# k transposed right after its convolution, with its norm, its decayed copy and v's scaling on ScalarE, and weight units in every other step of the down phase

## The chip, the cores and the metric

The kernel runs on one core of one Trainium2 chip. The metric is the device time of one execution in microseconds (us), as the median of several runs. A core has five engines with instruction streams of their own: TensorE (PE in the profile; its weight loads are PEld), VectorE (DVE), ScalarE (ACT), GpSimd (POOL) and SyncE (SP), which here issues nearly all transfers. Each engine and each queue does its instructions in order; semaphores order them against one another. Matrix products go to PSUM, which has eight banks of 128 x 512 float32.

## The reference

One layer of a hybrid decoder trunk on x of 1024 tokens by 1024 features, all in float32: a half SwiGLU feed-forward (FFN, inner width 2816), a mixer, a second FFN and a final norm. The mixer multiplies the normed x by one wide matrix w_in, runs eight GDN heads (gated delta rule, 128 wide) and sixteen Mamba-2 heads over the parts, and projects back with w_out. What matters here is a GDN head:

```python
def l2_normalize(x):
    return x * lax.rsqrt(jnp.sum(x * x, axis=-1, keepdims=True) + EPS)
...
    q = to_chunks(l2_normalize(q) * (dk ** -0.5))
    k = to_chunks(l2_normalize(k))
    v = to_chunks(v)
...
    decay = jnp.exp(jnp.where(incl, gc[..., :, None] - gc[..., None, :], -jnp.inf))
    kk = jnp.einsum("bhcld,bhcsd->bhcls", k, k)
    a_low = jnp.where(strict, beta[..., :, None] * kk * decay, 0.0)
    t_inv = lax.linalg.triangular_solve(eye + a_low, ...)
...
    k_dec = k * jnp.exp(gc[..., -1:] - gc)[..., None]
...
def step(state, inp):
    v_new = u_c - w_c @ state
    o = qd_c @ state + qk_c @ v_new
    state = state * gt_c + k_dec_c^T @ v_new
```

q, k and v come from projections of the normed x, each followed by a causal convolution of four taps and a SiLU. The last lines are abridged.

## The kernel before, in words

**Products.** Each float32 operand is split into a high and a low part of a TensorE format (`split`, L244: a cast on ScalarE, a subtraction on VectorE), and each product is three matmuls. The FFNs and part of the projections use a Strassen-like scheme of seven products on 2 x 2 blocks.

**Stages.** Norm and start, the first FFN's gate and up products, its down phase (about 454 to 660 us), gates and Mamba heads (to about 1000), GDN heads 0 to 7 (about 1000 to 1580), output projection, second FFN. The framework's scheduler orders every engine's instructions by a cost model of its own, so that work of neighbouring stages is interleaved; the order is fixed when the kernel is built.

**The down phase.** Class `Down` walks 42 steps, seven products of six steps. One step is up to 24 matmuls. `Down.prep` (L524) prepares a later step: it loads weight blocks (`wst`, or `keep` for blocks used more than once), loads the hidden activations (`hraw`, from the DRAM tile `hid_scr`), and splits both into `wd` and `hid`. Ahead of that, each call advances `self.side` by one: a generator, `win_units` (L653), that makes the weight units of GDN heads 4 to 7. It loads a column block of w_in (`wraw`), forms sums of its quarters (`wsum`), splits each of seven combinations into a unit (`wunit`) and writes the two halves to DRAM (`wu_scr`, two transfers of 256 KB). Six of eight column blocks are made in the gate and up phase, the last two here, which is fourteen units. At the second product the residual x is loaded (`xtb`, eight transfers of 512 KB). All of these stand in SP's one queue.

**A GDN head.** Heads 0 to 3 project q, k, v and the gate z with ordinary products; heads 4 to 7 do so with `chunk` (L1244), which loads the weight units back (`wunits`, by `unit_load`, L1230, four slots ahead). Then, in the order of the code, with NB = 8 blocks of 128 tokens:

- `kt`, `qt` and `vt_` are the convolved q, k, v, features in partitions, tokens in columns. `conv_from` ends in a SiLU on ScalarE.
- `qe` and `dt` are exponentials of the gates (L1357, L1360), of which each change of function on ScalarE costs a table load.
- For each pair of blocks a PSUM bank of tag `mx` (there are two) takes `kt`'s products with itself and with `qt` (L1372, L1373). VectorE takes the diagonal of the first by a product with the identity (`jd`, L1376), which is the squared norm of each k (`tk`), and then per pair `tk + EPS`, its reciprocal and `br2`. With that it makes `u` (L1383) and `dt` (L1386) out of the bank.
- `vt_` is transposed through `mx`, and VectorE scales it into `vr` (L1412).
- A forward substitution on small blocks follows (`fu`, `fx`, `lv`, L1429 to L1475).
- `kt` is transposed through the two banks of tag `sc` (L1486), and ScalarE scales it by the decay to the end of the chunk, `kd` (L1489, one buffer).
- The recurrence over the blocks (L1498 to L1520), its output norm, and a store `mix_scr` (L1532).

The output projection (`group_tile`, L1557) begins inside the last heads. Its bank copies are `xa` (L1566), its operands `mtt`.

Of the kernel before, what the change touches and what calls it, by code (L numbers as in the profile page):

```python
# [11 lines left out]
F32 = mybir.dt.float32  # L12
# [32 lines left out]
def kernel(  # L45
# [452 lines left out]
    class Down:  # L498
# [23 lines left out]
            return t  # L522

        def prep(self):  # L524
            next(self.side, None)
            if not self.todo:
                return
            m, i, n = self.todo.pop(0)
            c, self.cnt = self.cnt, self.cnt + 1
            raw = wp.tile([P, 2, 2, 512], F32, name="wst", tag="wst")  # L530
            x, *y = W_OPS[m]
            src = self.block(m, x, i, n, raw[:, 0])
            other = self.block(m, y[0], i, n, raw[:, 1]) if y else None
            hraw = hbp[0].tile([P, 2, 512], F32, name="hraw", tag=f"b{3 + c % 3}")
            nc.sync.dma_start(out=hraw[:, 0:n], in_=self.scr[m, i])
            if y:
                V.tensor_tensor(out=raw[:, 0, 0:n], in0=src, in1=other, op=y[1])
                src = raw[:, 0, 0:n]
            w = wp.tile([P, 2, 2, 512], F32R, name="wd", tag=("whi", "wlo")[c % 2])

            th = "b3" if self.tail > 3 and not self.todo else f"b{c % 3}"
            h = hbp[0].tile([P, 2, 2, 512], F32R, name="hid", tag=th)
            split(h[:, 0, 0:n], h[:, 1, 0:n], hraw[:, 0:n])
            self.last = split(w[:, 0, 0:n], w[:, 1, 0:n], src)
            self.ready.append((h, w, n))
# [423 lines left out]
    def token_sums(pool, sq, dst):  # L969

        p = psum("mx")
        for j in range(4):
            T.matmul(p[32 * j:32 * j + 32, 0:256], lhsT=ones[:, 0:32], rhs=sq[:, j * 256:(j + 1) * 256],
                     start=True, stop=True)
        row = pool.tile([P, 256], F32, name="row")
        A.copy(out=row, in_=p[:, 0:256])
        scr = dram.tile([4, 256], F32, name="row_scr", bufs=2)
        nc.sync.dma_start(out=scr, in_=row[0:P:32])
        nc.sync.dma_start(out=dst, in_=scr.rearrange("j (c p) -> p (j c)", p=P))
# [330 lines left out]
    with ExitStack() as cg:  # L1310
        g1 = cg.enter_context(tc.tile_pool(name="gdn1", bufs=1, reuse_waits="tile"))
        g2 = cg.enter_context(tc.tile_pool(name="gdn2", bufs=2, reuse_waits="tile"))
        for h in range(GH):
# [50 lines left out]
            u = g2.tile([P, NB, P], F32, name="u")  # L1364
            tk = g2.tile([P, NB], F32, name="tk")
            br2 = g2.tile([P, NB], F32, name="br2")
            for b0 in range(0, NB, 2):
                pg = psum("mx")
                b2 = slice(b0, b0 + 2)
                for i in range(2):  # L1370
                    bs = slice((b0 + i) * P, (b0 + i + 1) * P)
                    T.matmul(pg[:, i * 256:i * 256 + P], lhsT=kt[:, bs], rhs=kt[:, bs], start=True, stop=True)  # L1372
                    T.matmul(pg[:, i * 256 + P:(i + 1) * 256], lhsT=kt[:, bs], rhs=qt[:, bs],  # L1373
                             start=True, stop=True)
                    jd = g1.tile([P, P], BF16, name="jd")
                    V.scalar_tensor_tensor(out=jd, in0=pg[:, i * 256:i * 256 + P], scalar=1.0, in1=ident,  # L1376
                                           op0=ALU.mult, op1=ALU.mult,
                                           accum_out=tk[:, b0 + i:b0 + i + 1])
                V.tensor_scalar(out=tk[:, b2], in0=tk[:, b2], scalar1=EPS, scalar2=None, op0=ALU.add)
                V.reciprocal(out=br2[:, b2], in_=tk[:, b2])  # L1380
                V.tensor_tensor(out=br2[:, b2], in0=br2[:, b2], in1=beta[:, b2, h], op=ALU.mult)
                for i in range(2):
                    V.scalar_tensor_tensor(out=u[:, b0 + i], in0=pg[:, i * 256:i * 256 + P],  # L1383
                                           scalar=br2[:, b0 + i:b0 + i + 1], in1=dt[:, b0 + i],
# [21 lines left out]
            for half in range(2):  # L1406
                pt = psum("mx")
                for i in range(4):
                    b = half * 4 + i
                    T.transpose(pt[:, i * P:(i + 1) * P], vt_[:, b * P:(b + 1) * P], ident)  # L1410
                hb = slice(half * 4, half * 4 + 4)
                V.tensor_tensor(out=vr[:, hb], in0=pt.rearrange("p (i c) -> p i c", i=4),  # L1412
                                in1=rin[:, hb].unsqueeze(2).to_broadcast([P, 4, P]), op=ALU.mult)


            fs_x = dram.tile([4, NB, 32, 32], F32, name="fs_x", bufs=2)
# [15 lines left out]
            fs_q = fs_x.rearrange("j b (i q) l -> q (j b) i l", q=4)  # L1432
            for q in range(4):
                nc.sync.dma_start(out=fs_q[q], in_=fx[32 * q:32 * q + 32])
            lv = g1.tile([P, 4, 256], F32, name="lv")
            xd, xtr, mt = (lv[:, i].rearrange("p (b l) -> p b l", b=NB) for i in range(3))
            lv2 = g1.tile([P, 2, NB, 64], F32, name="lv2", tag="fu")
            x64, mt2 = lv2[0:64, 0], lv2[:, 1]
# [35 lines left out]
            for b in range(NB):  # L1474
# [1 line left out]
                         start=True, stop=True)  # L1476
            V.tensor_scalar(out=u[0:64, :, 64:128], in0=px[0:64].rearrange("p (b l) -> p b l", b=NB),
                            scalar1=-1.0, scalar2=None, op0=ALU.mult)


            kd = g1.tile([P, NB, P], F32, name="kd")
            for half in range(2):
                pt = psum("sc")
                for i in range(4):
                    b = half * 4 + i
                    T.transpose(pt[:, i * P:(i + 1) * P], kt[:, b * P:(b + 1) * P], ident)  # L1486
                for i in range(4):
                    b = half * 4 + i
                    A.mul(out=kd[:, b], in_=pt[:, i * P:(i + 1) * P], mul=wend[:, b, h:h + 1])  # L1489


            st = None
# [218 lines left out]
```

## Time and profile before

| | |
|---|---|
| median of 3 runs | 2324.86 us (2323.8 to 2327.96) |
| profiled execution | 2323.62 us, span 2321.9 us, mean granted TensorE clock 0.994 |
| TensorE busy | 2268.5 us (98% of the span) |
| VectorE busy | 1777.1 us (77%) |
| ScalarE busy | 1175.0 us (51%) |
| transfers | 356.96 MB, mean 154 GB/s |

TensorE's busy share is near the whole span, so the time is made of what TensorE does, of its few waits, and of stretches in which its granted clock is below 1. In the profile's rows an instruction shows as line, engine, operation and output<-inputs; what stands in brackets behind it is the engine's idle time just before and the instruction or transfer that ended it. SPq is SP's queue of transfers.

### The profile page before, as it was taken

The numbers are of one execution on the slowest core, as the hardware profiler recorded it, in microseconds if no ns is written. First come the engines' busy times: TensorE is split into PE (matmuls) and PEld (weight loads), VectorE is DVE, ScalarE is ACT, GpSimd is POOL, SyncE is SP. The second block draws the span as 40 slices with busy tenths as digits, with TensorE's granted clock in tenths as the row PEclk, the third lists the DMA queues.
The fourth block names the chain that finished last, engine by engine and source line by source line (L and its number), as shares of the span: only waits on it lengthen the run. The fifth ranks groups of instructions, "written<-read, shape, count | busy, mean of one in ns | idle before, by whom it ended". The sixth has DMA issues, their size and how long they took to land.

```text
span 2321.9 us, 32028 instructions
## 1 busy us (share of the span) xinstructions
PE 2268.5 (98%) x11654; PEld 1848.5 (80%) x11654; DVE 1777.1 (77%) x3417; ACT 1175.0 (51%) x2126; POOL 53.0 (2%) x125
## 2 busy tenths in 40 slices
PE   7999999989999999999999999999999999999998
PEld 5788888878878878887787777788878888888886
DVE  8998987768776887667667767678698777766787
ACT  7444433344366986864665566633453333334344
POOL 0000000000000110000000000000000000000000
PEclk9999999999999999999999999999999999999999
DMA  3466662595554433242355556435223333329455
GB/s 111 163 217 236 227 217 97 187 349 177 192 185 138 135 121 100 73 130 65 83 170 165 165 171 182 148 98 191 91 64 123 106 106 110 106 88 353 141 157 213
DMA packets 262195, 356.96 MB, mean 154 GB/s; under 512 B 60809, under 2 KB 167405, under 8 KB 260245
## 3 DMA queue, kind: packets, MB, share of 16 engines
q1 hardware_dynamic: 261780, 354.82, 46.9%
q8 instruction: 91, 1.49, 0.3%
q14 instruction: 68, 0.55, 0.1%
q0 software_dynamic: 256, 0.10, 0.0%
HBM read 249.34 MB, written 105.52 MB: 153 GB/s over the span
## 4 chain that ended last, share of the span: by engine, by line
PE 81%; DVE 7%; ACT 6%; DMA 3%; issue 1%; POOL 0%; SPq 0%; DVEq 0%; ACTq 0%; POOLq 0%
PE ps_pj L123 7%; PE ps_pj L125 7%; PE ps_pj L124 7%; PE ps_pj L334 6%; PE ps_pj L336 6%; PE ps_pj L335 6%; PE ps_mx L334 3%; PE ps_mx L336 3%; PE ps_mx L335 3%; PE ps_pj L559 2%; PE ps_pj L560 2%; PE ps_pj L558 2%; PE ps_oo L334 2%; PE ps_oo L335 2%; PE ps_oo L336 2%
## 5 line engine op out<-in xcount | busy, mean ns | idle before, releaser
L336 PE MATMUL ps_pj<-bh,al 128*128 128x512 f32 x688 | 267.9, 389 | 0.0
L334 PE MATMUL ps_pj<-bh,ah 128*128 128x512 f32 x688 | 267.7, 390 | 0.2 <-ACT m L343 0.2
L335 PE MATMUL ps_pj<-bl,ah 128*128 128x512 f32 x688 | 267.8, 389 | 0.0
L123 PE MATMUL ps_pj<-hhi,whi 128*128 128x512 f32 x576 | 229.9, 399 | 0.4 <-ACT gsb L896 0.4
L125 PE MATMUL ps_pj<-hhi,wlo 128*128 128x512 f32 x576 | 229.4, 398 | 0.0
L124 PE MATMUL ps_pj<-hlo,whi 128*128 128x512 f32 x576 | 228.9, 397 | 0.0
L336 PEld LDWEIGHTS ps_pj<-bh,al 128*128 128x128 f32 x688 | 129.1, 188 | 26.8
L335 PEld LDWEIGHTS ps_pj<-bl,ah 128*128 128x128 f32 x688 | 129.2, 188 | 26.8
L334 PEld LDWEIGHTS ps_pj<-bh,ah 128*128 128x128 f32 x688 | 128.9, 188 | 27.1 <-ACT m L343 0.6
L241 ACT CAST hid<-hraw 128x1024 fp32r<-128x1024 f32 (+1 forms) x84 | 82.3, 981 | 134.6 <-PE ps_oo L560 47.8
L242 DVE TENSOR_TENSOR al<-as,ah 128x512 fp32r<-128x512 f32 x220 | 140.9, 684 | 7.0 <-ACT ah L241 6.5
L317 DVE TENSOR_TENSOR as<-wst 128x512 f32<-128x512 f32 x220 | 144.2, 683 | 2.4 <-DMA wst<-in_ffn_w_up_dram 2.2
L334 PE MATMUL ps_mx<-bh,ah 128*128 128x512 f32 x352 | 138.6, 396 | 5.2 <-ACT sg L380 2.2
L241 ACT CAST ah<-wst 128x512 fp32r<-128x512 f32 x88 | 54.5, 622 | 174.8 <-PE ps_oo L335 112.6
L336 PE MATMUL ps_mx<-bh,al 128*128 128x512 f32 x352 | 137.7, 391 | 1.2 <-DVE al L242 1.2
L335 PE MATMUL ps_mx<-bl,ah 128*128 128x512 f32 x352 | 138.2, 393 | 0.5 <-DVE bl L242 0.5
L241 ACT CAST ah<-as 128x512 fp32r<-128x512 f32 x220 | 125.3, 618 | 20.8 <-DVE as L317 20.8
L123 PEld LDWEIGHTS ps_pj<-hhi,whi 128*128 128x128 f32 x576 | 108.4, 188 | 22.0 <-ACT gsb L896 0.8
L125 PEld LDWEIGHTS ps_pj<-hhi,wlo 128*128 128x128 f32 x576 | 108.4, 188 | 21.3 <-issue 0.9
L124 PEld LDWEIGHTS ps_pj<-hlo,whi 128*128 128x128 f32 x576 | 108.4, 188 | 21.0 <-issue 0.8
L242 DVE TENSOR_TENSOR hid<-hraw,hid 128x1024 fp32r<-128x1024 f32 (+1 forms) x84 | 95.0, 1131 | 23.2 <-ACT hid L241 22.8
L343 ACT COPY m<-ps_pj 128x512 f32<-128x512 f32 x88 | 51.5, 587 | 107.3 <-PE ps_pj L336 105.5
(507 smaller groups left out, 5651.5 us busy)
## 6 DMA issues: line engine op xcount, KB each, us to landing
hraw<-hid_scr SPq DMA_DIRECT2D x70, 512.0 KB, 4.3
wu_scr<-wunit SPq DMA_DIRECT2D x112, 256.0 KB, 3.9
wunits<-wu_scr SPq DMA_DIRECT2D x56, 512.0 KB, 3.9
hid_scr<-hs SPq DMA_DIRECT2D x110, 256.0 KB, 2.6
wst<-in_ffn_w_down_dram SPq DMA_DIRECT2D x50, 512.0 KB, 4.7
wst<-in_ffn_w_gate_dram SPq DMA_DIRECT2D x22, 1024.0 KB, 5.4
wst<-in_ffn_w_up_dram SPq DMA_DIRECT2D x22, 1024.0 KB, 5.5
hid_scr<-sg SPq DMA_DIRECT2D x44, 256.0 KB, 2.0
```

What stands on the lines that cost most here:

```text
L123: T.matmul(o, lhsT=wh, rhs=mh, start=first, stop=False)
L124: T.matmul(o, lhsT=wh, rhs=ml, start=False, stop=False)
L125: T.matmul(o, lhsT=wl, rhs=mh, start=False, stop=last)
L241: return (A.copy(out=hi, in_=src), V.tensor_tensor(out=lo, in0=src, in1=hi.bitcast(F32), op=ALU.subtract))
L242: V.tensor_tensor(out=lo, in0=src, in1=hi.bitcast(F32), op=ALU.subtract))
L317: V.tensor_tensor(out=t, in0=v[0], in1=v[1], op=v[2])
L334: T.matmul(bank, lhsT=wh[:, k], rhs=bh[:, k], start=a, stop=False, skip_group_check=True)
L335: T.matmul(bank, lhsT=wh[:, k], rhs=bl[:, k], start=False, stop=False, skip_group_check=True)
L336: T.matmul(bank, lhsT=wl[:, k], rhs=bh[:, k], start=False, stop=z, skip_group_check=True)
L343: A.copy(out=t, in_=bank)
L558: T.matmul(bank, lhsT=hh, rhs=wh, start=first and k == 0, stop=False, skip_group_check=True)
L559: T.matmul(bank, lhsT=hh, rhs=wl, start=False, stop=False, skip_group_check=True)
```

## The change

It has four parts.

1. `Down.prep` advances the generator of weight units only at every other step.
2. In each GDN head `kt` is transposed through `mx` as soon as it is convolved, ahead of its products. Of each transposed block ScalarE takes the squared norm (a Square with a sum on its output, which gives `tk`) and the decayed copy `kd`, which now has two buffers. `tk + EPS`, its reciprocal and `br2` are computed once for all eight blocks. VectorE's diagonal and the transposes through `sc` are gone.
3. `vr` is scaled on ScalarE, in eight pieces of 128 x 128 instead of two of 128 x 512 on VectorE.
4. The tile `row` of `token_sums` shares its buffer with `fx`, and `lv` has three slots instead of four.

```diff
--- before.py
+++ after.py
@@ -522,7 +522,8 @@
             return t
 
         def prep(self):
-            next(self.side, None)
+            if self.cnt % 2:
+                next(self.side, None)
             if not self.todo:
                 return
             m, i, n = self.todo.pop(0)
@@ -972,7 +973,7 @@
         for j in range(4):
             T.matmul(p[32 * j:32 * j + 32, 0:256], lhsT=ones[:, 0:32], rhs=sq[:, j * 256:(j + 1) * 256],
                      start=True, stop=True)
-        row = pool.tile([P, 256], F32, name="row")
+        row = pool.tile([P, 256], F32, name="row", tag="fx")
         A.copy(out=row, in_=p[:, 0:256])
         scr = dram.tile([4, 256], F32, name="row_scr", bufs=2)
         nc.sync.dma_start(out=scr, in_=row[0:P:32])
@@ -1364,6 +1365,20 @@
             u = g2.tile([P, NB, P], F32, name="u")
             tk = g2.tile([P, NB], F32, name="tk")
             br2 = g2.tile([P, NB], F32, name="br2")
+            kd = g1.tile([P, NB, P], F32, name="kd", bufs=2)
+            for half in range(2):
+                pt = psum("mx")
+                for i in range(4):
+                    b = half * 4 + i
+                    T.transpose(pt[:, i * P:(i + 1) * P], kt[:, b * P:(b + 1) * P], ident)
+                for i in range(4):
+                    b = half * 4 + i
+                    jd = g1.tile([P, P], BF16, name="jd")
+                    A.activation(out=jd, in_=pt[:, i * P:(i + 1) * P], func=AF.Square, accum_out=tk[:, b:b + 1])
+                    A.mul(out=kd[:, b], in_=pt[:, i * P:(i + 1) * P], mul=wend[:, b, h:h + 1])
+            V.tensor_scalar(out=tk, in0=tk, scalar1=EPS, scalar2=None, op0=ALU.add)
+            V.reciprocal(out=br2, in_=tk)
+            V.tensor_tensor(out=br2, in0=br2, in1=beta[:, :, h], op=ALU.mult)
             for b0 in range(0, NB, 2):
                 pg = psum("mx")
                 b2 = slice(b0, b0 + 2)
@@ -1372,13 +1387,6 @@
                     T.matmul(pg[:, i * 256:i * 256 + P], lhsT=kt[:, bs], rhs=kt[:, bs], start=True, stop=True)
                     T.matmul(pg[:, i * 256 + P:(i + 1) * 256], lhsT=kt[:, bs], rhs=qt[:, bs],
                              start=True, stop=True)
-                    jd = g1.tile([P, P], BF16, name="jd")
-                    V.scalar_tensor_tensor(out=jd, in0=pg[:, i * 256:i * 256 + P], scalar=1.0, in1=ident,
-                                           op0=ALU.mult, op1=ALU.mult,
-                                           accum_out=tk[:, b0 + i:b0 + i + 1])
-                V.tensor_scalar(out=tk[:, b2], in0=tk[:, b2], scalar1=EPS, scalar2=None, op0=ALU.add)
-                V.reciprocal(out=br2[:, b2], in_=tk[:, b2])
-                V.tensor_tensor(out=br2[:, b2], in0=br2[:, b2], in1=beta[:, b2, h], op=ALU.mult)
                 for i in range(2):
                     V.scalar_tensor_tensor(out=u[:, b0 + i], in0=pg[:, i * 256:i * 256 + P],
                                            scalar=br2[:, b0 + i:b0 + i + 1], in1=dt[:, b0 + i],
@@ -1408,9 +1416,9 @@
                 for i in range(4):
                     b = half * 4 + i
                     T.transpose(pt[:, i * P:(i + 1) * P], vt_[:, b * P:(b + 1) * P], ident)
-                hb = slice(half * 4, half * 4 + 4)
-                V.tensor_tensor(out=vr[:, hb], in0=pt.rearrange("p (i c) -> p i c", i=4),
-                                in1=rin[:, hb].unsqueeze(2).to_broadcast([P, 4, P]), op=ALU.mult)
+                for i in range(4):
+                    b = half * 4 + i
+                    A.mul(out=vr[:, b], in_=pt[:, i * P:(i + 1) * P], mul=rin[:, b:b + 1])
 
 
             fs_x = dram.tile([4, NB, 32, 32], F32, name="fs_x", bufs=2)
@@ -1432,7 +1440,7 @@
             fs_q = fs_x.rearrange("j b (i q) l -> q (j b) i l", q=4)
             for q in range(4):
                 nc.sync.dma_start(out=fs_q[q], in_=fx[32 * q:32 * q + 32])
-            lv = g1.tile([P, 4, 256], F32, name="lv")
+            lv = g1.tile([P, 3, 256], F32, name="lv")
             xd, xtr, mt = (lv[:, i].rearrange("p (b l) -> p b l", b=NB) for i in range(3))
             lv2 = g1.tile([P, 2, NB, 64], F32, name="lv2", tag="fu")
             x64, mt2 = lv2[0:64, 0], lv2[:, 1]
@@ -1476,17 +1484,6 @@
                          start=True, stop=True)
             V.tensor_scalar(out=u[0:64, :, 64:128], in0=px[0:64].rearrange("p (b l) -> p b l", b=NB),
                             scalar1=-1.0, scalar2=None, op0=ALU.mult)
-
-
-            kd = g1.tile([P, NB, P], F32, name="kd")
-            for half in range(2):
-                pt = psum("sc")
-                for i in range(4):
-                    b = half * 4 + i
-                    T.transpose(pt[:, i * P:(i + 1) * P], kt[:, b * P:(b + 1) * P], ident)
-                for i in range(4):
-                    b = half * 4 + i
-                    A.mul(out=kd[:, b], in_=pt[:, i * P:(i + 1) * P], mul=wend[:, b, h:h + 1])
 
 
             st = None
```

The number of TensorE's instructions stays the same; VectorE has 152 fewer instructions, and ScalarE has eight table loads fewer (66 instead of 74). The scheduler moves instructions on all engines from about the first down phase on. Two places show what moves.

SP's queue in the down phase, around the eight loads of the residual (`xtb`), before:

```order
L535 DMA hraw<-hid_scr_2_0_84 128x1024
L666 DMA wu_scr_169<-wunit 128x512 x2
L521 DMA keep_4235<-in_ffn_w_down_dram 128x2x512
L535 DMA hraw<-hid_scr_2_2_85 128x1024
L578 DMA xtb<-in_x_dram 128x1024 x8
L666 DMA wu_scr_169<-wunit 128x512 x2
L521 DMA keep_4326<-in_ffn_w_down_dram 128x2x512
L535 DMA hraw<-hid_scr_2_4_86 128x1024
L666 DMA wu_scr_169<-wunit 128x512 x2
L658 DMA wraw<-in_w_in_dram 128x8x128 x2
```

and now:

```order
L536 DMA hraw<-hid_scr_2_0_84 128x1024
L667 DMA wu_scr_169<-wunit 128x512 x2
L521 DMA keep_4215<-in_ffn_w_down_dram 128x2x512
L536 DMA hraw<-hid_scr_2_2_85 128x1024
L579 DMA xtb<-in_x_dram 128x1024 x8
L521 DMA keep_4296<-in_ffn_w_down_dram 128x2x512
L536 DMA hraw<-hid_scr_2_4_86 128x1024
L667 DMA wu_scr_169<-wunit 128x512 x2
L521 DMA keep_4296<-in_ffn_w_down_dram 128x2x512
L536 DMA hraw<-hid_scr_2_6_87 128x1024
```

The pair of writes to `wu_scr` behind the `xtb` loads is gone from there, and the load of the next column block, `wraw`, has left this piece. Before, from the end of the gate and up phase on (454 us), five pairs stood ahead of `hraw<-hid_scr_2_4_86`, three of them ahead of this piece; now one does.

ScalarE's stream in the set-up of head 7, before, with the start of v's convolution (`vt_`, L1268), table loads, `qe`, the two SiLUs (`zc` and `vt_`), the exponentials (`dt`, L1360) and the copies `xa` of the output projection:

```order
L1268 ACTIVATE vt__13353<-pre,cols 128x1024
L1264 COPY zc<-ps_pj 128x512
L1348 ACTIVATE zc<-zc 128x1024
L1357 ACT_TABLE_LOAD
L1357 ACTIVATE qe<-dt 128x1024
L1566 ACTIVATE xa<-ps_pj,rg_7158 128x512
L1270 ACT_TABLE_LOAD
L1270 ACTIVATE vt__13353<-vt__13353 128x1024
L1360 ACT_TABLE_LOAD
L1360 ACTIVATE dt<-dt,ngc 128x128 x8
L1566 ACTIVATE xa<-ps_pj,rg_7158 128x512
```

and now, where every line number is one higher up to the exponentials, L1377 are the squares and L1378 the decayed copies:

```order
L1269 ACTIVATE vt__13332<-pre,cols 128x1024
L1265 COPY zc<-ps_pj 128x512
L1358 ACT_TABLE_LOAD
L1358 ACTIVATE qe<-dt 128x1024
L1349 ACT_TABLE_LOAD
L1349 ACTIVATE zc<-zc 128x1024
L1271 ACTIVATE vt__13332<-vt__13332 128x1024
L1361 ACT_TABLE_LOAD
L1361 ACTIVATE dt<-dt,ngc 128x128 x8
L1377 ACTIVATE jd,tk<-ps_mx 128x128
L1378 ACTIVATE kd<-ps_mx,wend 128x128
```

Six of the eight blocks of k are squared and copied ahead of this piece, from the SiLU of `kt` on; one pair of square and copy stands at its end, behind the eight exponentials, and another follows. The copies `xa` have moved behind them. The SiLU of `zc` has moved behind `qe`, to that of `vt_`, and shares its table load.

On TensorE, 37 matmuls of weight units stand at that head between the last matmul of the recurrence before and the eight transposes of k; 24 more, the products of the first pair of blocks, and eighteen matmuls of the output projection stand between those and the products of the second pair.

## The prediction

> **What bounds the kernel.** I began with the page's busy shares and the chain that ended last, since they say which engine's time is the kernel's time.
>
> ```profile
> span 2321.9 us, 32028 instructions
> PE 2268.5 (98%) x11654; PEld 1848.5 (80%) x11654; DVE 1777.1 (77%) x3417; ACT 1175.0 (51%) x2126; POOL 53.0 (2%) x125
> PE 81%; DVE 7%; ACT 6%; DMA 3%; issue 1%; POOL 0%; SPq 0%; DVEq 0%; ACTq 0%; POOLq 0%
> ```
>
> TensorE is idle for 2321.9 − 2268.5 = 53.4 us of the whole program. The change keeps the number of its matmuls and transposes, so it can win only what lies in those idle times and in the slow clock behind them. The view of waits names them; the second and third columns of figures are how many times and the longest one.
>
> ```profile
> PE ps_sc L558 <- ACT hid L241: 5.4, 1, 5.4
> PE ps_mx L1372 <- DVE dt L1386: 3.7, 1, 3.7
> PE ps_pj L1239 <- DMA wunits<-wu_scr: 3.5, 1, 3.5
> PE ps_mx L1372 <- DVE jd L1376: 2.8, 5, 0.9
> ```
>
> The change touches all four places: the first is in the first down phase, the others are in the set-up of the GDN heads. The profiled execution took 2323.62 us, 1.7 more than its span and 1.24 below the median of the three runs; I make the sum against 2323.62 and add 1.24 at the end.
>
> **Part 1: a weight unit every other step of the down phase.** The views of TensorE, ScalarE and of SP's queue in time around the 5.4 us, with the stretches beside them (columns: length, busy time of PE, PEld, DVE, ACT, POOL, granted clock, DMA share, GB/s):
>
> ```profile
> 454.33 1.17 SPq L666 DMA_DIRECT2D wu_scr<-wunit  x2
> ...
> 477.64 9.03 SPq L578 DMA_DIRECT2D xtb<-in_x_dram  x8
> 487.68 1.61 SPq L666 DMA_DIRECT2D wu_scr<-wunit  x2
> 490.24 0.38 SPq L521 DMA_DIRECT2D keep<-in_ffn_w_down_dram  x1
> 491.47 0.32 SPq L535 DMA_DIRECT2D hraw<-hid_scr  x1
> 499.19 1.04 ACT L241 CAST wd<-keep 128x1024 fp32r<-128x1024 f32 x1 [10.16 <-DMA keep<-in_ffn_w_down_dram]
> 500.46 1.04 ACT L241 CAST hid<-hraw 128x1024 fp32r<-128x1024 f32 x1 [0.24 <-DMA hraw<-hid_scr]
> 495.79 0.39 PE L560 MATMUL ps_mx<-wd,hid 128*128 128x512 f32 x1
> 501.56 0.80 PE L558 MATMUL ps_sc<-wd,hid 128*128 128x512 f32 x1 [5.39 <-ACT hid L241]
> 506.96 0.40 PE L558 MATMUL ps_mx<-wd,hid 128*128 128x512 f32 x1
> wu_scr<-wunit SPq DMA_DIRECT2D x112, 256.0 KB, 3.9
> L242 DVE TENSOR_TENSOR wunit<-wsum,wunit 128x512 fp32r<-128x512 f32 x32 | 21.7, 686 | 1.3 <-DMA wu_scr<-wunit 1.2
> 477.60:500.40 22.80, 18.58 (x82) 15.04 (x81) 7.74 (x10) 8.24 (x12) 0.00 (x0) 0.99 1.03 392
> 530.00:610.00 80.00, 80.00 (x355) 66.24 (x354) 64.23 (x72) 28.93 (x31) 0.00 (x0) 1.00 0.49 155
> ```
>
> The stall is a transfer that comes late, not a busy ScalarE: ScalarE sat 10.16 us before the cast of wd and then waited for hraw, and all DMA engines were full (share 1.03). Five pairs of wu_scr writes stand on SP between 454.33 and 487.68 ahead of this hraw. In the changed order one pair of these is left ahead of it, so 4 × 2 × 256 KB = 2.1 MB go later. At 392 GB/s that is 5.35 us: hraw lands at 500.46 − 5.35 = 495.1, the matmul follows as now 501.56 − 500.46 = 1.1 us later, at 496.2. Full-speed pitch is 80.00/355 = 0.225 us, so it is wanted at 495.79 + 0.23 = 496.0, and a stall of 0.2 is left. What the stall costs now is more than 5.39: from 495.79 to 506.96 twelve matmuls start ahead of the last, 13 steps that need 2.9 us at full pitch, and they took 11.17. Gain 8.2; I take **−8.0**. The nearest bound below: were only two of the four pairs of consequence, 2.7 us of wait would be left and about half of the gain, −3. None at all is a rival below.
>
> What is moved comes back between 500 and 610 us, where DMA is at a share of 0.49 and TensorE never waits. VectorE's part of a unit goes there too: a sum and a subtraction of 0.69 each, about 10 us for the seven of the fourteen units that are late; VectorE has 80 − 64.2 = 15.8 us free there. I cost it at 0; it would be 0 to +2 if a write that waits for its unit holds a later hraw in SP's queue, which is in order.
>
> **Part 2: ScalarE takes the norm and the decayed copy; head 7.** Prices first: VectorE's diagonal (L1376), VectorE's scaling of v (L1412), ScalarE's decayed copy (L1489), and ScalarE's square with sum on the output (L1526), the nearest row for the new square of k.
>
> ```profile
> L1376 DVE SCALAR_TENSOR_TENSOR jd<-ps_mx,ident x64: 268/284/292, 1016.1 to 1463.0; 128x128 bf16<-128x128 f32 x64
> L1412 DVE TENSOR_TENSOR vr<-ps_mx,rin x16: 680/691/692, 1029.0 to 1477.5; 128x512 f32<-128x512 f32 x16
> L1489 ACT ACTIVATE kd<-ps_sc,wend x64: 359/371/415, 1081.4 to 1545.3; 128x128 f32<-128x128 f32 x64
> L1526 ACT ACTIVATE jk<-vr x64: 294/310/320, 1084.7 to 1569.8; 128x128 bf16<-128x128 f32 x64
> L1526 ACT ACTIVATION_READ_ACCUMULATOR jk<-vr x64: 185/186/212, 1084.9 to 1570.0; 128x1 f32 x64
> 1010.00:1480.00 470.00, 457.44 (x3029) 364.31 (x3028) 341.73 (x1173) 279.38 (x606) 19.32 (x69) 0.99 0.48 136
> ```
>
> Per head ScalarE gains 8 × (0.310 + 0.186) = 4.0 us of squares and 8 × 0.371 = 3.0 of scalings of v; the decayed copies are moved, not added. VectorE loses 8 × 0.284 + 2 × 0.691 = 3.7 us and some small instructions. On average there is room: ScalarE is busy 279 of 470 us, and 56 us more makes 335. The average doesn't decide; the place does. Before, kk was multiplied at once and VectorE took the diagonal. Now kk needs a bank of ps_mx that is free only after four squares and four copies on ScalarE, behind whatever else stands there. That is worst at head 7, where ScalarE is full already. Head 7's set-up, and two rows from head 4's:
>
> ```profile
> 1430.22 0.41 PE L1509 MATMUL ps_oo<-vn,dt 128*128 128x128 f32 x2
> 1450.04 0.39 PE L125 MATMUL ps_pj<-w,mtt 128*128 128x512 f32 x1
> 1454.11 0.46 PE L1372 MATMUL ps_mx<-kt 128*128 128x128 f32 x2 [3.69 <-DVE dt L1386]
> 1439.07 1.98 ACT L241 CAST w<-x 128x1024 fp32r<-128x1024 f32 x2
> 1442.78 1.16 ACT L1268 ACTIVATE vt__13353<-pre,cols 128x1024 f32<-128x1024 f32 x1 [1.73 <-DVE pre L1262]
> 1443.95 0.59 ACT L1264 COPY zc<-ps_pj 128x512 f32<-128x512 f32 x1
> 1444.57 1.07 ACT L1348 ACTIVATE zc<-zc 128x1024 f32<-128x1024 f32 x1
> ...
> 1450.97 1.28 ACT L1360 ACT_TABLE_LOAD   x1
> 1452.27 2.45 ACT L1360 ACTIVATE dt<-dt,ngc 128x128 f32<-128x128 f32 x8
> 1452.70 0.94 DVE L1383 SCALAR_TENSOR_TENSOR u<-ps_mx,br,dt 128x128 f32<-128x128 f32 x3 [1.92 <-ACT dt L1360]
> 1450.00:1470.00 20.00, 16.31 (x160) 12.29 (x159) 10.98 (x37) 15.75 (x33) 0.28 (x1) 0.74 0.25 78
> 1236.59 0.57 SPq L1532 DMA_DIRECT2D mix_scr<-vr  x1
> 1237.27 2.77 SPq L1230 DMA_DIRECT2D wunits<-wu_scr  x2
> ```
>
> TensorE stood until VectorE had freed ps_mx, and VectorE had waited for the eight exponentials (1452.27), which came late on ScalarE. In the changed order the same ScalarE stretch also holds the squares and copies, and the last two blocks stand *behind* the exponentials. TensorE does 37 matmuls from the end of the last recurrence step before the eight transposes: 1430.4 + 37 × 0.225 = 1438.7, first square at about 1439.3. From there to the last copy ScalarE's order has 8 squares with their sums (3.97), 8 copies (2.97), two casts (1.98), the convolution's start for v (1.16), one copy of zc (0.59), three table loads (3.84), qe and two SiLUs (each like the SiLU of zc, 3.21) and the exponentials (2.45): 20.17 us, end at 1459.4. The second pair of blocks of kk waits for that; before it TensorE has 24 weight-unit matmuls, 4 small ones and 18 of the output projection, and runs out of work near 1450.6. Idle 8.8 instead of 3.7: **+5.1**. Bounds: +0, if the group of v (casts and zc) comes as much earlier as the squares take; +8, if the slow clock afterwards grows in proportion to the idle time, as 2.8 us (8.2 − 5.4) behind 5.39 in part 1 would make it 0.5 us per us.
>
> On that last point the Trainium skill ("TensorE: Matmul & The Clock Gate", Part 1) says that one idle window of some 3.4 us halves the clock and as long a busy stretch restores it; then 8.8 us idle would cost no more clock than 3.7, and the term stays +5.1 rather than +7.7. The trace agrees so far as the two waits above each have a slow stretch behind them (clock 0.74 over 1450 to 1470).
>
> **Part 3: the other heads.** The five jd waits (2.8 us) can't recur as such, but kk now waits for ScalarE instead of VectorE, and in five heads this takes the place of a wait of 0.9 or less. Bounds −2.8 to +4 (eight heads at +0.5); I take **−1**, since VectorE, busier than ScalarE (341.7 against 279.4), is relieved. The 3.5 us for wunits at head 4 I cost at 0: that load stands on SP behind the store mix_scr (1236.59), which waits for ScalarE's last scalings of the head before, and it stands there in the new order too. The transposes of k leave ps_sc in the recurrence's start for ps_mx earlier: same instructions, 0. The fx memset on POOL now waits also for the row transfers, which end before the heads; 0.
>
> Sum: 2323.62 − 8.0 + 5.1 − 1 = 2319.7, and 1.24 more is 2320.9 on the scale of the median; I say 2320.5.
>
> **Rivals.** 0.2% of this time, 4.65 us, is about what a measurement can tell from no change: faster is below 2320.2, slower above 2329.5.
>
> (a) *Head 7 doesn't grow.* The relief of VectorE brings v's convolution and zc forward, and the squares fill the 1.73 us that ScalarE waited for pre at 1442.78. Then the whole part 1 is kept: 2323.62 − 8 − 1 − (0 to 4, if the 3.7 goes too) + 1.24 = 2312 to 2316. Against it: two of the eight blocks stand behind the exponentials in ScalarE's order.
>
> (b) *ScalarE becomes the bound in every head's set-up; slower.* TensorE waits in each head from the transposes to the first bank's release: 4 × (0.496 + 0.371) = 3.5 us, less some 1.5 us of small work beside it. Where ScalarE takes up the squares at once, projections cover this; where it is behind by more than they last, each of eight heads pays about 2: +16 in all, with −8 from part 1 and +1.24, 2333; with six heads, 2329. It decides when ScalarE is more than 3 us behind at the transposes in most heads. For it: one such place at head 7 by the order; against it: 190 us of ScalarE's 470 are free.
>
> The Trainium skill ("ScalarE: Activation LUTs", Rules for kernel authors) says to give plain multiplications to VectorE, not ScalarE. The rows agree on engine time: 4 × 0.371 = 1.48 us for a half of v against 0.691.
>
> (c) *Part 1 brings nothing.* hraw comes late in any case, held by keep and xtb (8 loads, 9.03 us), or a later hraw is held by a delayed write: 2323.62 + 5.1 − 1 + 1.24 = 2329. Against it: 2.1 MB leave a full DMA stretch.
>
> **Chances.** Forecast 0.45 (own range 2316 to 2325; 0.21 of it faster, 0.24 same), (a) 0.26 (all faster), (b) 0.17 (all slower), (c) 0.12 (0.08 same, 0.04 slower). Faster 0.21 + 0.26 = 0.47, same 0.24 + 0.08 = 0.32, slower 0.17 + 0.04 = 0.21. The range takes (a) in nearly whole and reaches to (c) and the low end of (b): 2310 to 2329.
>
> **What would show it.** Right: no ps_sc wait for hid near 495 us, the down phase 8 us shorter; at head 7 a wait of ps_mx for kd of 7 to 10 us; wunits at head 4 again about 3.5; heads 0 to 3 and 5 unchanged within 1 us each. Wrong: waits for kd of over 1.5 us in most heads (b); hid waited for near 496 or at a later step (c); no wait at head 7 over 4 us (a).

## The result, and the profile after

The changed kernel takes 2317.55 us (median of 8 runs, 2314.44 to 2320.58) against 2322.41 us before (8 runs, 2321.74 to 2327.96). The ratio is 0.9975, 95% interval 0.9964 to 0.9986: 0.25% faster, or 5.8 us by the ratio. The profiled execution took 2316.89 us, 6.7 less than the one before.

The page of the changed kernel: span, busy times, chain.

```profile
span 2315.2 us, 32011 instructions
PE 2263.0 (98%) x11654; PEld 1845.1 (80%) x11654; DVE 1743.0 (75%) x3201; ACT 1197.1 (52%) x2310; POOL 52.8 (2%) x125
PE 78%; DVE 9%; ACT 8%; DMA 3%; issue 2%; POOL 0%; SPq 0%; DVEq 0%; ACTq 0%; POOLq 0%
```

VectorE lost 34 us and ScalarE took 22 more, as the change says. The page counts 216 instructions fewer on VectorE, not 152, because the trace lists the read of each of the 64 sums of the old diagonal as a record of its own. TensorE's busy time fell by 5.5 us with the same number of instructions: about half of that (2.8 us) because less of its work ran at half clock (13.0 us of busy time against 18.7), most of the rest because some matmuls of the heads stand closer together (below). Its idle time is 52.2 us, against 53.4: the waits were exchanged more than removed. From the view of waits, what is new (us in total, times, longest):

```profile
PE ps_mx L1387 <- ACT kd L1378: 8.2, 3, 7.0
...
PE ps_pj L1240 <- ACT kt L1269: 3.0, 1, 3.0
...
PE ps_pj L1240 <- ACT qt L1271: 1.6, 1, 1.6
```

The wait for hid (5.4) is gone. The place that was predicted for a longer wait, head 7, has one of 7.0 for `kd`.

**The down phase.** SP and ScalarE in time around the old stall, changed kernel:

```profile
474.59 6.66 SPq L579 DMA_DIRECT2D xtb<-in_x_dram  x8
482.25 0.38 SPq L521 DMA_DIRECT2D keep<-in_ffn_w_down_dram  x1
484.50 0.33 SPq L536 DMA_DIRECT2D hraw<-hid_scr  x1
493.49 1.05 ACT L241 CAST wd<-keep 128x1024 fp32r<-128x1024 f32 x1 [6.35 <-DMA keep<-in_ffn_w_down_dram]
494.71 1.05 ACT L241 CAST hid<-hraw 128x1024 fp32r<-128x1024 f32 x1 [0.17 <-DMA hraw<-hid_scr]
```

The transfer lands 5.75 us earlier on the trace's own time (494.71 against 500.46), although this trace runs 1.3 us late ahead of it. SP issues it 7.0 us earlier (484.50 against 491.47): the eight loads of the residual take 6.66 us to issue instead of 9.03, and the pair of writes behind them is gone. ScalarE still waits for the transfer, but TensorE doesn't. The stretches of time in the trace before (length, busy time of PE, PEld, DVE, ACT, POOL, granted clock, DMA share, GB/s); the first holds the old stall, the others are used below:

```profile
480.00:520.00 40.00, 34.58 (x142) 27.65 (x141) 21.31 (x24) 19.67 (x25) 0.00 (x0) 0.91 1.01 371
1240.00:1250.00 10.00, 6.83 (x23) 5.48 (x24) 9.48 (x26) 6.80 (x11) 0.68 (x2) 0.83 0.30 104
1455.50:1465.70 10.20, 10.20 (x93) 8.20 (x94) 4.11 (x15) 7.15 (x11) 0.00 (x0) 0.50 0.01 4
```

The same of the changed kernel:

```profile
480.00:520.00 40.00, 40.00 (x178) 33.14 (x177) 23.70 (x26) 21.67 (x28) 0.00 (x0) 1.00 0.92 333
1444.00:1454.20 10.20, 6.22 (x52) 5.38 (x52) 4.95 (x20) 10.16 (x24) 0.00 (x0) 0.50 0.15 56
99.00:102.50 3.50, 3.50 (x10) 2.73 (x9) 3.50 (x7) 3.36 (x7) 0.00 (x0) 0.51 0.19 27
```

In the 40 us of the first row TensorE starts 178 matmuls instead of 142, and the clock is full.

**Head 7.** ScalarE and TensorE in its set-up, changed kernel:

```profile
1429.95 0.28 ACT L1377 ACTIVATE jd<-ps_mx 128x128 bf16<-128x128 f32 x1
1430.12 0.20 ACT L1377 ACTIVATION_READ_ACCUMULATOR jd<-ps_mx 128x1 f32 x1
1430.21 0.36 ACT L1378 ACTIVATE kd<-ps_mx,wend 128x128 f32<-128x128 f32 x1
1430.47 0.28 ACT L1377 ACTIVATE jd<-ps_mx 128x128 bf16<-128x128 f32 x1
...
1435.85 1.15 ACT L1269 ACTIVATE vt__13332<-pre,cols 128x1024 f32<-128x1024 f32 x1 [0.79 <-DVE pre L1263]
...
1444.46 2.45 ACT L1361 ACTIVATE dt<-dt,ngc 128x128 f32<-128x128 f32 x8
1446.81 0.26 ACT L1377 ACTIVATE jd<-ps_mx 128x128 bf16<-128x128 f32 x1
...
1447.56 0.36 ACT L1378 ACTIVATE kd<-ps_mx,wend 128x128 f32<-128x128 f32 x1
1440.60 0.39 PE L125 MATMUL ps_pj<-w,mtt 128*128 128x512 f32 x1
1447.98 0.80 PE L1387 MATMUL ps_mx<-kt 128*128 128x128 f32 x2 [6.99 <-ACT kd L1378]
```

The last two pairs of square and copy stand behind the exponentials, as the order said; TensorE starts 0.06 us after the last copy ends. No table load stands between the exponentials and the squares, so not every change of function costs one here.

**Where the time went, in one table.** For each kernel the k-th matmul of each source line is matched with the k-th of the same line before; the columns are how much the difference of the two start times (median over a stretch) grows in a stage. "Idle" is TensorE's idle time over the GDN heads and the start of the output projection (1000 to 1600 us), "half" the time in that stretch in which the trace's record of the granted clock says one half, and "busy in half" TensorE's busy time within it. Work at half clock costs half its time extra, so the last column but one, idle + busy in half / 2, is what the stretch loses by waits and clock. All in us, one profiled execution each.

| kernel | to 470 | down stall | 545 to 1000 | heads and projection | idle | half | busy in half | lost | ratio to before, 95% |
|---|---|---|---|---|---|---|---|---|---|
| before | | | | | 12.6 | 13.7 | 13.7 | 19.4 | |
| changed | +1.3 | −8.4 | +0.8 | −0.5 | 16.4 | 13.7 | 9.5 | 21.1 | 0.9975, 0.9964 to 0.9986 |
| e1_down_only | +1.3 | −8.2 | +1.0 | −1.8 | 12.6 | 10.2 | 10.2 | 17.7 | 0.9969, 0.9956 to 0.9981 |
| e2_gdn_only | +0.9 | +0.8 | +0.4 | +0.2 | 17.0 | 13.7 | 9.3 | 21.6 | 1.0002, 0.9994 to 1.0011 |
| e3_xtb_spread | +2.1 | −6.6 | +0.3 | −0.1 | 12.7 | 13.7 | 13.7 | 19.5 | 0.9970, 0.9959 to 0.9982 |
| e4_norm_on_vector | +0.5 | −8.4 | +0.9 | −3.5 | 16.1 | 6.8 | 3.4 | 17.8 | 0.9959, 0.9947 to 0.9972 |
| e5_v_on_vector | 0.0 | −8.4 | +0.5 | +1.6 | 17.1 | 20.5 | 15.4 | 24.8 | 0.9973, 0.9961 to 0.9984 |
| e6_k_first | +2.0 | −8.3 | 0.0 | +0.5 | 16.6 | 10.2 | 10.2 | 21.7 | 0.9970, 0.9959 to 0.9980 |
| e7_exps_first | +0.8 | −8.4 | +1.0 | +7.4 | 17.0 | 17.1 | 16.2 | 25.1 | 0.9998, 0.9989 to 1.0007 |
| e8_after_exps_first | +3.2 | −8.3 | −0.1 | −12.7 | 9.1 | 0.0 | 0.0 | 9.1 | 0.9929, 0.9916 to 0.9943 |
| e9_norm_vec_exps_first | +2.1 | −8.2 | +0.1 | +13.1 | 23.9 | 23.9 | 18.5 | 33.1 | 1.0031, 1.0021 to 1.0041 |
| e10_exps_store_act | +1.4 | −8.6 | +0.5 | +1.7 | 17.5 | 6.8 | 6.5 | 20.7 | 0.9984, 0.9975 to 0.9993 |
| e11_after_exps_store_act | +1.8 | −7.5 | −0.7 | +1.3 | 17.0 | 10.2 | 10.0 | 22.0 | 0.9977, 0.9966 to 0.9988 |
| e12_down_store_act | +1.7 | −8.0 | +0.5 | +3.5 | 14.9 | 17.1 | 15.8 | 22.8 | 0.9994, 0.9985 to 1.0003 |

For the changed kernel: −8.4 + 0.8 − 0.5, and +1.3 at the start, where a stretch at half clock at 99 us (last row of the windows above) alone costs 1.7, far ahead of anything that the change touches. So the gain is the down phase, and the heads come out even.

They don't come out even by waiting less. In e1 and e3 the loss by waits and clock differs from before as the time does (−1.7 and −1.8, +0.1 and −0.1). In the changed kernel the loss grows by 1.7 us and the time falls by 0.5. The 2.2 us between are work at full clock: from start to start, the 64 matmuls of `token_sums` in the heads (sums over the features, as products with ones) take 7.8 us before and in e1, 5.6 in the changed kernel and in e2. Where TensorE's order keeps the eight of a head together, they take about as long as two that it parts from the rest. An example of each, before and changed:

```profile
1076.30 0.62 PE L973 MATMUL ps_mx<-qsq,ones 128*32 128x256 f32 x2
1071.72 0.64 PE L974 MATMUL ps_mx<-qsq,ones 128*32 128x256 f32 x8
```

### The profile page after: what moved, and what is told of

Read it like the earlier page. It is cut to its first block, busy times and chain, and to the rows that moved or that the text cites. A ratio compares the mean times of both kernels' runs of the same rounds, so it can differ in the third digit from the quotient of the medians.

```text
span 2315.2 us, 32011 instructions
## 1 busy us (share of the span) xinstructions
PE 2263.0 (98%) x11654; PEld 1845.1 (80%) x11654; DVE 1743.0 (75%) x3201; ACT 1197.1 (52%) x2310; POOL 52.8 (2%) x125
## 4 chain that ended last, share of the span: by engine, by line
PE 78%; DVE 9%; ACT 8%; DMA 3%; issue 2%; POOL 0%; SPq 0%; DVEq 0%; ACTq 0%; POOLq 0%
PE ps_pj L123 6%; PE ps_pj L125 6%; PE ps_pj L124 6%; PE ps_pj L334 6%; PE ps_pj L335 6%; PE ps_pj L336 6%; PE ps_mx L336 3%; PE ps_mx L334 3%; PE ps_mx L335 3%; PE ps_pj L1240 2%; PE ps_oo L334 2%; PE ps_oo L335 2%; PE ps_pj L1241 2%; PE ps_oo L336 2%; PE ps_pj L560 2%
```

## The experiments

**The two parts apart.** e1_down_only is the kernel before with the one line of the down phase; e2_gdn_only is the changed kernel without it.

```diff
         def prep(self):
-            next(self.side, None)
+            if self.cnt % 2:
+                next(self.side, None)
```

> The kernel before with only the down-phase line changed (a weight unit every other step). Theory A, the gain of the change is the transfer that no longer comes late: the ps_sc wait for hid near 495 us (5.4) is gone, no slow clock near 500 to 507, and the time is 8 us (7 to 9) below before, about 3 below the changed kernel's median. Rival, part of the gain comes from the relieved VectorE in the heads: at most 4 us below before.

> The changed kernel with a weight unit in every step again, so only the heads are changed. Theory A: the wait for hid near 495 us is back at 5 to 6 us, TensorE's wait at head 7 is for kd and 6 to 9 us, and the time is within 2 us of before, since what head 7 loses the other heads win. Rival, the head 7 wait costs what it was forecast to: 3 to 6 us slower than before.

Measured: e1_down_only 2317.37 us against 2325.62 before on the same chip, 0.31% faster (7.2 us by the ratio, 4 to 10 by its interval); e2_gdn_only 2325.59, no difference (1.0002). From e1's windows, the old stall and head 4:

```profile
480.00:520.00 40.00, 40.00 (x178) 33.16 (x177) 24.44 (x28) 22.33 (x29) 0.00 (x0) 1.00 0.92 332
1240.00:1250.00 10.00, 9.50 (x45) 7.60 (x44) 5.19 (x16) 5.75 (x11) 1.13 (x7) 1.00 0.41 101
```

and from e2's waits:

```profile
PE ps_mx L1386 <- ACT kd L1377: 8.4, 3, 7.0
...
PE ps_sc L558 <- ACT hid L241: 5.7, 2, 5.2
```

The down line alone gives what the whole change gives; the heads alone give nothing, in spite of 7.0 us of wait at head 7. What theory A forecast came in both. Its reason for e2, that the other heads win what head 7 loses, holds only so far as the matmuls of `token_sums` stand closer together: idle and half clock lose 2.2 us more there than before. Its aside that e1 would be 3 us below the changed kernel isn't shown: the two ratios, 0.9969 and 0.9975, can't be told apart.

**Is it bandwidth ahead of hraw?** e3_xtb_spread leaves the units in every step and takes the other large user out of the way:

```diff
-            if m == 2:
-                for b in range(NB):
-                    nc.sync.dma_start(out=xt[b], in_=x_src[:, b])
...
                 dn.prep()
+                if m in (2, 5) and loads:
+                    b = loads.pop(0)
+                    nc.sync.dma_start(out=xt[b], in_=x_src[:, b])
```

> The kernel before with weight units in every step, but the eight loads of the residual (4.2 MB) issued one per step of the second and third product instead of at once. If the stall near 495 us is DMA bandwidth ahead of hraw, whoever uses it, hraw lands up to 10 us earlier, the wait is under 1 us and the time 7 to 9 us below before. If it is the units' own work or their waiting writes in SP's queue, a wait of 4 us or more stays and the time is within 3 us of before.

```profile
480.00:520.00 40.00, 39.67 (x174) 32.54 (x175) 28.03 (x33) 24.63 (x34) 0.00 (x0) 1.00 1.04 387
```

0.30% faster, with the units' work and their writes where they were. DMA is still full in this stretch (share 1.04), but hraw is no longer behind 4.2 MB, and TensorE waits for hid no longer than 0.3 us between 450 and 560 us. So the stall goes with what stands ahead of hraw, whoever it belongs to. Both edits also take instructions out of SP's queue ahead of hraw; issuing the same bytes from another queue at the same time would tell the two apart, and wasn't tried. For the bytes speak the 5.35 us that the prediction worked out from them, against 5.75 measured.

**What the head 7 wait is made of.** e6_k_first writes the transposes, squares and copies ahead of v's projection; e4_norm_on_vector leaves the norm on VectorE (the old diagonal) with the early copies; e5_v_on_vector gives v's scaling back to VectorE.

```diff
# e6_k_first
                 conv_from(pre[1], 8 + h, kt)
+                kd, tk, br2 = k_prep(kt, h)
# e4_norm_on_vector
-                    A.activation(out=jd, in_=pt[:, i * P:(i + 1) * P], func=AF.Square, accum_out=tk[:, b:b + 1])
...
+                    V.scalar_tensor_tensor(out=jd, in0=pg[:, i * 256:i * 256 + P], scalar=1.0, in1=ident, ...
# e5_v_on_vector
-                    A.mul(out=vr[:, b], in_=pt[:, i * P:(i + 1) * P], mul=rin[:, b:b + 1])
+                V.tensor_tensor(out=vr[:, hb], in0=pt.rearrange("p (i c) -> p i c", i=4), ...
```

> The changed kernel with the transposes of k, the squares and the copies written ahead of v's projection, so that in ScalarE's order of head 7 all eight pairs stand ahead of the start of v's convolution and of the exponentials. If the head 7 wait is ScalarE's order, TensorE's wait for kd there is under 2 us and the time 2 to 5 us below the changed kernel, 8 to 11 below before. Rival, the wait moves to what is pushed back (v, the exponentials, the weight units): some other wait of 3 us or more at head 7, and no better than the changed kernel.

> The changed kernel with the norm of k on VectorE as before (the diagonal of its product), while the transposes and decayed copies stay early. If ScalarE's squares are what the head 7 wait is made of, it falls under 4 us and the time by 2 to 4 us against the changed kernel. If it is the place of ScalarE's exponentials among the copies, a wait of 5 us or more for kd stays at head 7 and the time is within 2 us of the changed kernel, 4 to 9 below before.

> The changed kernel with the scaling of v back on VectorE (2 instructions of 128x512 per head). If VectorE's relief from it pays, 2 us or more slower than the changed kernel; if ScalarE's 3 us per head for it cost, 2 us or more faster; by the theory that both are hidden behind TensorE, within 2 us of the changed kernel.

e6's waits over the heads:

```profile
PE ps_pj L1240 <- DMA wunits<-wu_scr: 5.9, 3, 2.9
PE ps_mx L1323 <- ACT kt L858: 3.7, 3, 1.6
PE ps_mx L1323 <- ACT kt L1271: 2.0, 2, 1.2
```

The wait for kd at head 7 is gone, as ScalarE's order says, but others came: idle 16.6 against 16.4, and the time (0.9970) can't be told from the changed kernel's. The rival came true in its sum, though mostly at other heads and with no wait over 2.9. e4 at 0.9959 is some 4 us better than the changed kernel by the two ratios, with intervals that overlap; its wait at head 7 stays:

```profile
PE ps_mx L1382 <- DVE dt L1396: 5.3, 1, 5.3
PE ps_pj L1240 <- DMA wunits<-wu_scr: 3.5, 3, 1.5
```

Each branch of its expectation was half right: the wait stayed over 5 us (for `dt`, not for kd), and the time came down all the same, by less work at half clock (3.4 us against 9.5). e5 is as fast as the changed kernel, as was expected, but not because v's scaling is hidden either way. Its waits over the heads:

```profile
PE ps_sc L1478 <- ACT lv L1471: 4.3, 1, 4.3
PE ps_sc L1457 <- DVE lv L1451: 3.6, 2, 2.6
...
PE ps_mx L1387 <- ACT kd L1378: 1.4, 3, 0.7
```

The wait for kd at head 7 is gone, though the squares and copies are as they were, and TensorE waits there for `lv` of the forward substitution, with 17.1 us at half clock. By the table the heads take 2.1 us more than in the changed kernel and the start 1.3 less. The equal time hides two different orders, and what the scaling itself costs isn't shown.

**The exponentials first.** e7_exps_first and e8_after_exps_first move one block of code ahead of each head's projections; e7 does it in e1_down_only, e8 in the changed kernel.

```diff
             vt_ = g1.tile([P, L], F32, name="vt_")
+            qe = g2.tile([P, L], F32, name="qe")
+            dt = g2.tile([P, NB, P], F32, name="dt")
+            nc.sync.dma_start(out=dt, in_=g_scr[h]. ...
+            A.activation(out=qe, in_=dt.rearrange("p b t -> p (b t)"), func=AF.Exp)
+            causal(dt, (NB,))
+            for b in range(NB):
+                A.activation(out=dt[:, b], in_=dt[:, b], func=AF.Exp, bias=ngc[:, b, h:h + 1])
```

> The kernel before with the down-phase line (as e1_down_only) and the exponentials qe and dt written ahead of the projections of each head, so that ScalarE does them ahead of k's and v's SiLU. If the head 7 wait of before is ScalarE's late exponentials, it falls under 1 us, the half-clock stretch behind it (10.2 us) goes or shortens, and the time is 5 to 8 us below e1_down_only: 2309 to 2313, 0.5 to 0.65% below before. Rival, the wait moves to the SiLU of k or to the weight units: within 2 us of e1_down_only.

> The changed kernel with the exponentials written ahead of the projections in the same way. If the order of ScalarE alone makes the 7 us wait for kd at head 7, it falls under 3 us and the time by 3 to 7 us against the changed kernel. If squares and copies are too much for ScalarE there in any order, a wait of 4 us or more stays and the time is within 2 us of the changed kernel.

e7's waits over the heads, then e8's:

```profile
PE ps_pj L1240 <- DMA wunits<-wu_scr: 10.7, 4, 3.4
```

```profile
PE ps_mx L1387 <- ACT kd L1378: 2.0, 2, 1.9
PE ps_pj L1240 <- ACT kt L1269: 2.0, 1, 2.0
PE ps_pj L1240 <- ACT zc L1260: 1.9, 1, 1.9
PE ps_pj L1240 <- ACT pre L1256: 1.2, 1, 1.2
```

e8 is the version that beats both: 2307.52 us against 2323.69, 0.71% faster. The wait at head 7 is 1.9 instead of 7.0, no wait in the heads is over 2.0, and the half clock is gone from the whole stretch, which is why it won 10.7 us more than the change (0.46% between the ratios) and not the 3 to 7 expected. In e7 the head 7 wait of before (3.7) went too, but waits for the weight units stand at heads 4 to 7 (1.3, 3.4, 3.2 and 2.7 us), each with half clock behind it, and all that e1 had won is lost: worse than both branches.

**Is it the store on SP's queue?** The prediction put the 3.5 us for wunits at head 4 down to the store `mix_scr` ahead of the load. Three kernels issue that store from ScalarE's queue: e12 in e1, e10 in e7, e11 in e8. A fourth, e9, puts e4's edit into e8.

```diff
-            nc.sync.dma_start(out=mix_scr[h // 2]...
+            nc.scalar.dma_start(out=mix_scr[h // 2]...
```

> e1_down_only with the store mix_scr from ScalarE's queue. By the queue theory the wait for wunits at head 4 (3.5 us) goes and with it the slow clock that may stand behind it: 3 to 6 us below e1, 0.45 to 0.6% below before. If the load there waits for its buffer, the wait stays and the time is within 1.5 us of e1.

> e7_exps_first (no gain, four waits of 2 to 3.4 us for wunits) with only the store mix_scr issued from ScalarE's queue instead of SP's. If those waits come from wunits loads standing behind that store on SP, which waits for ScalarE's last scalings, at most one wait for wunits over 1 us is left and the time is 8 to 15 us below before. If the loads are late for their buffers or for bandwidth, the four waits stay and the time is within 3 us of before.

> e8_after_exps_first with the store mix_scr from ScalarE's queue. e8 has only 0.3 us of waits for wunits, so by the queue theory within 2 us of e8; any larger gain would show that the store holds SP's queue there too.

> e8_after_exps_first with the norm of k on VectorE (as in e4_norm_on_vector), so that ScalarE has 4 us per head less. If squares on ScalarE cost in the heads whatever the order, 2 to 5 us below e8's 0.7% gain, 0.8 to 0.95% below before. If with the exponentials first they are hidden, within 2 us of e8.

e12's wait at head 4:

```profile
1237.72 0.47 PE L1240 MATMUL ps_pj<-hhi,wunits 128*128 128x512 f32 x1 [3.40 <-DMA wunits<-wu_scr]
```

With the store off SP the wait is still 3.40. The store isn't its cause. In the changed kernel the same matmul waits 3.02 for ScalarE's start of k's convolution instead; in the trace before, that instruction ended at 1242.82 (1241.69 + 1.13) and the matmul started at 1243.17. So two releasers, as what ends a wait is called here, come within 0.4 us of one another there, and to take one away leaves the other; what makes the load late isn't settled. e12 as a whole lost what e1 had won (0.9994; 5.8 us above e1, where the branch with the wait had said 1.5 at most), by half clock and by waits of up to 3.3 for jd at other places. e10 has three waits for wunits left (5.3, longest 2.9) and is 0.16% faster than before: against the queue theory, if better than e7. e11 is 0.5% slower than e8, and e9, two edits that had each come out well, is 1.0% slower than e8:

```profile
PE ps_mx L1373 <- ACT kt L1271: 7.7, 2, 4.8
PE ps_pj L1240 <- ACT pre L1254: 6.0, 2, 4.8
PE ps_pj L1240 <- DMA wunits<-wu_scr: 5.8, 3, 2.6
```

The expectations of e11 and e9, within 2 us of e8 or better, missed by 11 and 23 us. Every edit in the heads has the scheduler order the four engines anew, and the waits turn up elsewhere. That the order alone, and not the edit's own instructions, makes these differences is argued from the waits; it wasn't tried with the order held fixed.

## Why the prediction was right, step by step

- **Part 1, −8.0:** shown. The stall vanished at −8.4 by matched matmuls, e1 alone brings the gain, e2 alone doesn't, and e3 does it with another user's bytes. Of the 0 to +2 for what comes back later, 0.8 came. Rival (c) is out.
- **Head 7, +5.1:** the mechanism was right, the size wasn't. The wait is 6.99 and not 8.8. Counted from the first square, TensorE ran out of work after 11.0 us, where the sum had 11.3; the last copy ended after 18.0 us, where it had 20.2. So what was mis-sized is the pair of square and copy: the sum took 0.496 + 0.371 = 0.87 us a pair, and the trace shows the next pair 0.52 us behind (1429.95 to 1430.47), since the instructions overlap. The eight pairs took 4.3 us instead of 6.9, with 0.8 back for a wait for `pre`. Then the clock: both kernels have 10.2 us at half clock there, but before TensorE was busy in all of it, and now in 6.2; the longer wait lies partly in the slow stretch and cost 2.0 us less of it. By matched matmuls from before the set-up to behind it the head is some 2 us later, not 5.1; idle and half clock alone make it 1.4 (9.4 us before, 10.8 now).
- **On the slow clock,** the page "TensorE: Matmul & The Clock Gate" of the Trainium skill (Part 1) was the better guide than proportion: 7.0 us idle brought no longer stretch at half clock than 3.7. The traces agree with it on the step too: every stretch at half clock in these runs is a multiple of 3.41 us long, except the last one, which the end of the run cuts off, and the clock is 1.00 or 0.50 and nothing between. They don't agree that a busy stretch of that length restores the clock: before, TensorE was busy in all of the 10.2 us at half clock at head 7. 74 of the 93 matmuls there are of 32x32 or 64x64; whether their size is the reason wasn't tried.
- **The other heads, −1:** −0.5 over the whole stretch less the 2 of head 7 makes about −2.5, within the bounds given, but by luck: the reason given, VectorE's relief, doesn't show. The five waits for jd (2.8 us) are gone, others have come, and idle and half clock outside head 7 are 10.0 us before and 10.3 now. What was won is the 2.2 us of `token_sums`, which the prediction doesn't have. Forecast for all heads was +4.1, measured −0.5, and 0.0 ± 0.1% in e2. Rival (a) is out, since head 7's wait did grow, and so is (b): the waits for kd are 8.2 in three times, and 7.0 of it is head 7, so the other heads have 1.2 between them.
- **Head 4, 0:** the wait stayed about as long (3.0 us, now for ScalarE's `kt`, against 3.5), but the reason given, the store on SP, is refuted by e12.
- **v's scaling:** the Trainium skill's advice to keep multiplications on VectorE ("ScalarE: Activation LUTs", Rules for kernel authors) is neither borne out nor contradicted by the time: e5 follows it and is as fast (0.9973 against 0.9975), with other waits.
- The total came out near the forecast (0.19% forecast, 0.25% measured) partly by luck: the heads' error of 4.6 us was in part offset by the 1.3 us that the start lost and by 0.8 us that came back after the down phase.

## What to carry to other kernels

Price a stall on a transfer by the bytes ahead of it while DMA is full (here 5.35 us worked out, 5.75 measured), and move whichever are easiest to move. Where a kernel that is changed in one place gains in another, ask whether its waits are shorter there or its order only packs better. Add up an engine's work by the pitch of its instructions in a row (from one start to the next), not by their durations, and ask of a wait in the middle of dense TensorE work not only how long it is but whether it is long enough to bring the slow clock; getting all waits in the heads to 2 us or less was worth more here than their sum (e8 against the changed kernel: 7.3 us less idle, 12.2 us less time). Where a scheduler orders the whole stage, single edits there don't add, so compare whole builds, and read the waits of each.

## What the runs showed of the hardware

- The same wait can cost a stretch at half clock or not. At head 4, before and e1 have the same wait for wunits, 3.5 us; before runs at 0.83 of full clock over 1240 to 1250, e1 at 1.00 (both rows are above), which is 1.7 us for the moment at which the wait falls. The lengths of the stretches at full clock in the trace before (477.87, 737.28, 208.21, 849.92 us) are multiples of 3.413 too, to within 0.01 us, so the decision seems to be taken on a grid that runs on through the program. The Trainium skill's page on the clock gate (Part 1) says the same of the window ("free-running"). Laid on that grid, the wait before puts 2.71 us of idle time into one window, and e1's is cut into 1.68 and 1.79. Over all fourteen traces (40 to 2270 us), each of the 43 windows at full clock with 1.88 us or more of idle time is followed by half clock, 4 of the 13 with 1.66 to 1.82 are, and 1 of the 9020 with less. So about 1.9 us of the 3.41 was enough; the window didn't have to be idle throughout. It is one reason why runs of one kernel differ by a few us: of the 27 runs of the kernel before in the last round, the three with a mean clock of 0.992 took 2325.0 to 2326.0 us, the two with 0.996 took 2319.5 and 2320.9.
- Matmuls of `token_sums`, each with 32 columns of output, start 6 or 7 ns apart within a group of four; two that stand alone between other matmuls take 0.24 and 0.31 us from start to start.
- A ScalarE square with a sum on its output and a copy that follow one another start 0.52 us apart as a pair, where their three durations add up to 0.84 (0.28 + 0.20 + 0.36).
